# A decoder layer's opening: x scaled and transposed with the identity, first adaLN sums on TensorE, silu(c) later

## The chip, the core and the metric

The kernel runs on one core of a Trainium2 chip. The metric is the device time of one execution in microseconds. The trace names the engines PE (TensorE matmul; PEld its weight loads), DVE (VectorE), ACT (ScalarE), POOL (GpSimd) and SP (SyncE, which issues the transfers here). All data are float32, or float32 in the form that TensorE multiplies in fewer passes (`fp32r`).

## The reference, cut to what matters

One layer, 512 tokens, width 2048, batch 1. The part that the change touches is the modulated norm at its start:

```python
mod = jax.nn.silu(c) @ w_ada + b_ada                 # (1, 6144)
shift, scale, gate = jnp.split(mod[:, None, :], 3, axis=-1)
h = rms_norm(x, norm_w) * (1.0 + scale) + shift      # (1, 512, 2048)
proj = h @ w_in
```

Behind it stand sliding-window attention with sinks, a gated DeltaNet branch, their merge, and `x + gate * (y @ w_out)`. All of these read `proj`, and so `h`; the change does not touch them.

## The kernel before, in words

`startup` makes `h` transposed, 16 blocks of 128 channels by 512 tokens, and multiplies each block as soon as it is there with the first weights (`w_st`: two v tiles, one for beta and alpha, four k tiles). Its steps:

- **Loads.** SP issues all transfers in program order. x comes in four groups of 128 tokens (`xt`), the row of c spread over all partitions (`scb`, printed as `silu_cb`), the adaLN weights (`wa`) two tiles of 1 MiB for each block: `loads[kt, 0]` for shift and `loads[kt, 1]` for scale. `xt` and `wa` share six buffers, so a `wa` load can wait for an earlier tile to be used up. The weights `raw` have two buffers of their own.
- **Norm and transpose.** For each token group ScalarE squares x and sums (L467), VectorE takes the root of the mean in ten small instructions (L469 and `rsqrt`, L64), scales the identity by it into `dg` (L472), and TensorE multiplies x by `dg`, which scales and transposes in one (L477). VectorE and ScalarE in turn copy the result out of PSUM into `xnT` (L480, L482).
- **silu(c).** `silu(c)` in column form (`scr`) is the stationary operand for TensorE. The row form `scb` is made after the second group by a tanh on ScalarE (L486) and one instruction on VectorE (L487).
- **adaLN sums** (`ada_sums`, L420). For an even block the shift comes from 16 small TensorE matmuls (L428), a copy (L433) and a small matmul with `pick` (L434); the weights are laid out by `layout` for that. All others are dot products on VectorE (L437), 2.28 us each.
- **h** (`adaln`, L441). Two small VectorE instructions make shift and scale (`sh`, L445 and L449), ScalarE makes `h` (L454) and its high part `hh` (L455), VectorE the low part `hl` (`low`, L458).
- **Products.** Each weight half is split in the same way into `whi` (L61) and `wlo` (L62). `mm3` multiplies high by high, low by high and high by low (L255 to L257), so a block has 21 matmuls.

The loop over blocks `kt` (L504) writes down, in this order: `adaln(kt+1)`, the loads of block kt+3, the sums of block kt+2, `low(kt+1)`, the products of block kt. The order on each engine is not this order: a planner in the framework takes instructions by priority as they become ready by its own costs, and then each engine runs its list in order. `behind` (L259) adds an edge that makes the planner put one instruction after another on the same engine, without a wait at run time. After the loop the stage `delta_keys` begins, whose matmuls are named `mm`.

Of the kernel before, what the change touches and what calls it, by code (L numbers as in the profile page):

```python
# [7 lines left out]
F32 = mybir.dt.float32  # L8
F32R = mybir.dt.float32r
I32 = mybir.dt.int32  # L10
AF = mybir.ActivationFunctionType
ALU = mybir.AluOpType
# [4 lines left out]
P = 128  # L17
T = 512
D = 2048
KT = D // P  # L20
NTB = T // P
EPS = 1e-6
# [23 lines left out]
class Layer:  # L46
# [321 lines left out]
    def startup(self, st):  # L368


        tc, nc, a, const = self.tc, self.nc, self.a, self.const
        sp = st.enter_context(tc.tile_pool(name="st1", bufs=1, reuse_waits="tile"))
        s2 = st.enter_context(tc.tile_pool(name="st2", bufs=2, reuse_waits="tile"))
        pa = st.enter_context(tc.tile_pool(name="st_acc", bufs=1, space=PSUM, reuse_waits="tile"))
        acc, loads = {}, {}

        def load_ada(kt):
            for j in range(2):
                wa = s2.tile([P, D], F32, tag="wa", name="wa", bufs=6)
                nc.sync.dma_start(out=wa, in_=a["w_ada_ss"][kt, j])  # L380
                loads[kt, j] = wa

        consts = self.consts()
        xts = []
        scb = sp.tile([P, D], F32, name="silu_cb")
        for tb in range(NTB):
            xt = s2.tile([P, D], F32, tag="wa", name="xt", bufs=6)
            nc.sync.dma_start(out=xt, in_=a["x"][tb * P : (tb + 1) * P, :])
            xts.append(xt)
            if tb < 2:  # L390
                next(consts)
            if tb == 1:
                nc.sync.dma_start(out=scb, in_=a["c_row"].partition_broadcast(P))
        load_ada(0)
        next(consts)
        self.prime()
        load_ada(1)
        load_ada(2)
        next(consts)
# [6 lines left out]
        scr = sp.tile([P, KT, 32], F32, name="silu_cr")  # L406
        nc.vector.tensor_copy(out=scr, in_=self.sc.unsqueeze(2).to_broadcast([P, KT, 32]))
        pick = sp.tile([P, 1], F32, name="pick")
        nc.vector.memset(pick, 0.0)
        for g in range(4):  # L410
            nc.vector.memset(pick[32 * g : 32 * g + 1], 1.0)
        bn = sp.tile([P, KT], F32, name="bn")
        nc.vector.scalar_tensor_tensor(
            out=bn, in0=self.b_ada[:, KT : 2 * KT], scalar=1.0, in1=self.norm_w, op0=ALU.add, op1=ALU.mult
        )
        ssq = sp.tile([P, NTB], F32, name="xssq")
        xnT = sp.tile([P, KT, T], F32, name="xnT")
        ada = pa.tile([P, T], F32, name="ada")

        def ada_sums(kt):  # L420


            t = acc[kt] = s2.tile([P, 2], F32, tag="acc", name="acc")
            if kt % 2 == 0:
                w = loads[kt, 0].rearrange("p (k n) -> p k n", k=KT)
                for k in range(4):
                    for g in range(4):
                        nc.tensor.matmul(  # L428
                            ada[32 * g : 32 * g + 32, 0:P], lhsT=scr[:, 4 * k + g, :], rhs=w[:, 4 * k + g, :],
                            start=k == 0, stop=k == 3,  # L430
                        )
                sb = s2.tile([P, P], F32, tag="adas", name="adas", bufs=1)
                nc.scalar.copy(out=sb, in_=ada[:, 0:P])  # L433
                nc.tensor.matmul(ada[:, P : P + 1], lhsT=sb, rhs=pick, start=True, stop=True)  # L434
            for j in range(1 - kt % 2, 2):
                wa = loads[kt, j]
                nc.vector.scalar_tensor_tensor(  # L437
                    out=wa, in0=wa, scalar=0.5, in1=scb, op0=ALU.mult, op1=ALU.mult, accum_out=t[:, j : j + 1]
                )

        def adaln(kt):  # L441

            t = acc[kt]
            sh = s2.tile([P, 2], F32, tag="sh", name="sh")
            nc.vector.tensor_scalar(  # L445
                out=sh[:, 0:1], in0=t[:, 0:1] if kt % 2 else ada[:, P : P + 1], scalar1=self.b_ada[:, kt : kt + 1],
                scalar2=None, op0=ALU.add,
            )
            nc.vector.tensor_scalar(  # L449
                out=sh[:, 1:2], in0=t[:, 1:2], scalar1=self.norm_w[:, kt : kt + 1], scalar2=bn[:, kt : kt + 1],  # L450
                op0=ALU.mult, op1=ALU.add,
            )
            h32 = s2.tile([P, T], F32, tag="h32", name="h32")
            nc.scalar.activation(h32, xnT[:, kt, :], AF.Identity, scale=sh[:, 1:2], bias=sh[:, 0:1])  # L454
            nc.scalar.copy(out=self.hh[:, kt, :], in_=h32)  # L455
            return h32

        def low(kt, h32):  # L458
            nc.vector.tensor_tensor(
                out=self.hl[:, kt, :], in0=h32, in1=self.hh[:, kt, :].bitcast(F32), op=ALU.subtract  # L460
            )

        n = 0
        for tb in range(NTB):
            xt = xts[tb]
            junk = self.hl[:, 4 * tb : 4 * tb + 4, :].rearrange("p k t -> p (k t)")
            nc.scalar.activation(junk, xt, AF.Square, accum_out=ssq[:, tb : tb + 1])  # L467
            ms = sp.tile([P, 1], F32, tag="ms", name="ms", bufs=2)
            nc.vector.tensor_scalar(out=ms, in0=ssq[:, tb : tb + 1], scalar1=1.0 / D, scalar2=EPS, op0=ALU.mult, op1=ALU.add)  # L469
            r = self.rsqrt(sp, ms, 1, "xr")  # L470
            dg = s2.tile([P, P], F32, tag="dg", name="dg")
            nc.vector.tensor_scalar(out=dg, in0=self.ident, scalar1=r, scalar2=None, op0=ALU.mult)  # L472
            for q in range(4):
                i = n % 7
                ps = pa.tile([P, 4, P], F32, tag=f"x{i}", name="xtp") if i < 3 else self.psc.tile([P, 4, P], F32, tag="sc", name="xtp")
                for c in range(4):
                    nc.tensor.matmul(ps[:, c, :], lhsT=xt[:, (4 * q + c) * P : (4 * q + c + 1) * P], rhs=dg, start=True, stop=True)  # L477
                dst = xnT[:, 4 * q : 4 * q + 4, tb * P : (tb + 1) * P]
                if q % 2:
                    nc.vector.tensor_copy(out=dst, in_=ps)  # L480
                else:
                    nc.scalar.copy(out=dst, in_=ps)  # L482
                n += 1
            if tb == 1:
                thb = sp.tile([P, D], F32, name="silu_t")
                nc.scalar.activation(thb, scb, AF.Tanh, scale=0.5)  # L486
                nc.vector.scalar_tensor_tensor(out=scb, in0=thb, scalar=1.0, in1=scb, op0=ALU.add, op1=ALU.mult)  # L487

        def products(kt, parts):
            f, l = kt == 0, kt == KT - 1  # L490
            wh, wl = parts
# [3 lines left out]

        ada_sums(0)
        low(0, adaln(0))
        ada_sums(1)
        acc_v = [pa.tile([P, T], F32, tag=f"x{i}", name=f"v{i}") for i in range(2)]
        acc_ba = pa.tile([2 * VH, T], F32, tag="x2", name="ba")  # L500
# [1131 lines left out]
def layout(i):  # L1632
# [8 lines left out]
    o["c_row"] = f(i["c"].reshape(D))  # L1641
    ss = w_ada[:, : 2 * D].T.reshape(2, KT, P, D).transpose(1, 0, 2, 3).copy()
    ss[0::2, 0] = ss[0::2, 0].reshape(-1, P, KT, P).transpose(0, 3, 2, 1).reshape(-1, P, D)
    o["w_ada_ss"] = ss
    o["w_ada_gate"] = f(w_ada.reshape(KT, P, 3, D)[:, :, 2])
    o["b_ada"] = f(i["b_ada"][0].reshape(48, P).T)
# [65 lines left out]
```

## Time and profile before

| what | us |
|---|---|
| median of 3 runs | 2878.47 (2870.41 to 2881.5) |
| profiled execution | 2872.04, span 2870.2 |
| first matmul of a transposition (L477) | 10.27 |
| first product of block 0 (L255) | 32.93 |
| first product of block 1 | 41.54 |
| first product of block 2 | 48.30 |
| first product of block 15 | 136.46 |
| first `mm` of the next stage | 141.38 |

The positions are counted from the start of the span. Names are those of the program without buffer numbers. In a timeline a row gives start, duration, engine, line, operation, written and read tile, shapes, a count, and in brackets the idle time before it with what ended it. Durations of matmuls are modelled and overlap, so the spacing of their starts is the better measure.

### The profile page before, as it was taken

To read this page: it belongs to the slowest core of one execution; us is meant where nothing else is said; L and a number is where in the kernel's file an instruction comes from. 1 tells how busy PE (TensorE), PEld (TensorE's weight loads), DVE (VectorE), ACT (ScalarE), POOL (GpSimd) and SP (SyncE) were. 2 spreads that over 40 slices of the span, in tenths; PEclk is the share of its full clock that TensorE was granted. 3 is DMA by queue.
4 is the path that set the end of the run, shared out by engine and by line. 5 is a ranking of instruction groups with operands and counts; after the bars stand their busy time and mean duration, and the time that the engine had idled before them with its cause. 6 is when DMAs were issued, how large, how long until landed. Compare 5 with 4: busy or idle time off the path is not lost.

```text
span 2870.2 us, 38671 instructions
## 1 busy us (share of the span) xinstructions
PE 2820.4 (98%) x14396; PEld 2314.6 (81%) x14396; DVE 1969.6 (69%) x3174; ACT 1188.4 (41%) x2382; POOL 141.6 (5%) x124
## 2 busy tenths in 40 slices
PE   7899999999999999999999999999999999999999
PEld 6588888877877778888788888888888888878887
DVE  7776776868768766778676666665656776664576
ACT  4356443234444343433433333333334454433443
POOL 0001000100001000001000000000000000000000
PEclk9999999999999999999999999999999999999999
DMA  9777864322252343456777676666646887885784
GB/s 398 289 250 235 257 231 143 112 89 90 80 159 81 110 151 99 134 170 233 236 261 246 229 241 232 235 236 228 231 171 226 288 314 258 295 281 175 245 317 165
DMA packets 227727, 604.28 MB, mean 211 GB/s; under 512 B 76081, under 2 KB 102193, under 8 KB 187089
## 3 DMA queue, kind: packets, MB, share of 16 engines
q1 hardware_dynamic: 227538, 601.81, 62.0%
q8 instruction: 113, 1.85, 0.3%
q14 instruction: 76, 0.62, 0.1%
HBM read 481.32 MB, written 118.17 MB: 209 GB/s over the span
## 4 chain that ended last, share of the span: by engine, by line
PE 87%; DVE 5%; DMA 3%; ACT 2%; issue 1%; SPq 0%; POOL 0%; DVEq 0%; POOLq 0%; ACTq 0%
PE mm L255 20%; PE mm L257 20%; PE mm L256 20%; PE m L256 5%; PE m L255 5%; PE m L257 5%; DVE wa L437 1%; DVE wlo L62 1%; PE pv L933 1%; DMA E<-g_rows 1%; PE S L1389 1%; PE pod L952 1%; PE O L1440 1%; PE pP L296 1%; ACT sm L1413 1%
## 5 line engine op out<-in xcount | busy, mean ns | idle before, releaser
L255 PE MATMUL mm<-hh,whi 128*128 128x512 f32 x2784 | 1130.1, 406 | 2.8 <-ACT mth L285 2.8
L257 PE MATMUL mm<-hh,wlo 128*128 128x512 f32 x2784 | 1089.5, 391 | 0.0
L256 PE MATMUL mm<-hl,whi 128*128 128x512 f32 x2784 | 1086.9, 390 | 0.0
L62 DVE TENSOR_TENSOR wlo<-raw,whi 128x1024 fp32r<-128x1024 f32 (+1 forms) x532 | 655.2, 1232 | 425.0 <-ACT whi L61 409.6
L61 ACT CAST whi<-raw 128x1024 fp32r<-128x1024 f32 (+1 forms) x532 | 555.4, 1045 | 848.6 <-PE mm L256 612.2
L255 PEld LDWEIGHTS mm<-hh,whi 128*128 128x128 f32 x2784 | 523.5, 188 | 113.6 <-issue 9.2
L257 PEld LDWEIGHTS mm<-hh,wlo 128*128 128x128 f32 x2784 | 522.6, 188 | 113.6 <-issue 0.5
L256 PEld LDWEIGHTS mm<-hl,whi 128*128 128x128 f32 x2784 | 524.0, 188 | 100.4 <-issue 1.4
L1198 DVE TENSOR_TENSOR q<-q,q 128x1024 f32<-128x1024 f32 x96 | 124.5, 1297 | 0.2 <-DMA q<-in_w_od 0.2
L748 ACT ACTIVATE E<-E,neg_g 128x128 f32<-128x128 f32 x256 | 82.1, 393 | 88.7 <-POOL E L742 88.6
L777 DVE TENSOR_TENSOR atmp<-A 128x62 f32<-128x62 f32 (+30 forms) x124 | 109.7, 884 | 0.5
L785 DVE TENSOR_TENSOR A<-A,atmp 128x62 f32<-128x62 f32 (+30 forms) x124 | 109.1, 880 | 0.4
L880 POOL TENSOR_TENSOR qe<-qe,yq 128x512 f32<-128x512 f32 x32 | 50.9, 1608 | 940.2 <-DMA qe<-eg_rows 624.3
L953 ACT COPY osb<-pod 128x256 f32<-128x256 f32 x64 | 23.8, 372 | 149.9 <-PE pod L952 149.9
L742 POOL TENSOR_SCALAR_AFFINE_SELECT E<-E 128x512 f32<-128x512 f32 x64 | 60.0, 950 | 430.7 <-DMA E<-g_rows 307.2
L935 ACT COPY vn<-pv 128x256 f32<-128x256 f32 x64 | 23.8, 372 | 120.8 <-PE pv L933 120.8
L1413 ACT ACTIVATE sm<-sm,mx,rs 128x256 f32<-128x256 f32 (+1 forms) x128 | 71.7, 562 | 3.5 <-DVE mx L1408 3.5
L604 DVE SCALAR_TENSOR_TENSOR yv<-mm,convh,yv 128x511 f32<-128x511 f32 (+2 forms) x96 | 71.4, 743 | 1.2
L940 DVE TENSOR_SCALAR vs<-vn,kd 128x128 f32<-128x128 f32 x96 | 23.1, 283 | 60.6 <-ACT vn L935 60.6
L437 DVE SCALAR_TENSOR_TENSOR wa<-wa,silu_cb 128x2048 f32<-128x2048 f32 x24 | 54.8, 2283 | 0.0
L963 DVE SCALAR_TENSOR_TENSOR S<-S,egl,pod 128x128 f32<-128x128 f32 x64 | 19.3, 343 | 50.8 <-ACT junk L956 50.8
L609 ACT ACTIVATE th<-yv 128x512 f32<-128x512 f32 x32 | 20.1, 628 | 72.7 <-DVE yv L604 72.7
(427 smaller groups left out, 3684.4 us busy)
## 6 DMA issues: line engine op xcount, KB each, us to landing
raw<-in_w_ch SPq DMA_DIRECT2D x158, 1024.0 KB
wa<-in_w_ada_ss SPq DMA_DIRECT2D x32, 1024.0 KB
q<-in_w_od SPq DMA_DIRECT2D x64, 512.0 KB
g_d<-q SPq DMA_DIRECT2D x64, 512.0 KB
raw<-g_d SPq DMA_DIRECT2D x32, 1024.0 KB
raw<-in_w_od SPq DMA_DIRECT2D x24, 1024.0 KB
gw<-in_w_ada_gate SPq DMA_DIRECT2D x16, 1024.0 KB
E<-g_rows SPq DMA_DIRECT2D x64, 256.0 KB
```

The costliest lines, as they stand in the source:

```text
L61: self.nc.scalar.copy(out=hi, in_=src)
L62: self.nc.vector.tensor_tensor(out=lo, in0=src, in1=hi.bitcast(F32), op=ALU.subtract)
L255: nc.tensor.matmul(ps, lhsT=wh, rhs=xh, start=first, stop=False)
L256: nc.tensor.matmul(ps, lhsT=wh, rhs=xl, start=False, stop=False)
L257: self.last_mm = nc.tensor.matmul(ps, lhsT=wl, rhs=xh, start=False, stop=last)
L437: nc.vector.scalar_tensor_tensor(out=wa, in0=wa, scalar=0.5, in1=scb, op0=ALU.mult, op1=ALU.mult, accum_out=t[:, j : j + 1])
L604: nc.vector.scalar_tensor_tensor(out=y[:, s:], in0=ps[:, : T - s], scalar=w[:, j : j + 1], in1=y[:, s:], op0=ALU.mult, op1=ALU.add)
L748: self.nc.scalar.activation(E[:, c, :], E[:, c, :], AF.Exp, bias=self.neg_g[:, c, h : h + 1])
L777: eng.tensor_tensor(out=t, in0=A[:, m : m + 1, m + 1 :].to_broadcast([P, m, n]), in1=A[:, :m, m : m + 1].to_broadcast([P, m, n]), op=ALU.mult,
L785: self.behind(eng.tensor_tensor(out=A[:, :m, m + 1 :], in0=A[:, :m, m + 1 :], in1=t, op=ALU.add))
L1198: self.behind(nc.vector.tensor_tensor(out=q[f], in0=q[x], in1=q[y], op=ALU.add))
L1413: nc.scalar.activation(t, t, AF.Exp, scale=r[:, h : h + 1], bias=mx[:, h : h + 1], accum_out=den[:, h : h + 1])
```

## The change

- The row of c is loaded after the first two weight loads instead of after the second x group; `b_ada` and `norm_w` are loaded ahead of the first `wa`.
- Two token groups share one chain for the root. x itself is scaled in its buffer by VectorE, and TensorE transposes it with the unscaled identity. PSUM of groups 2 and 3 is copied out by ScalarE alone.
- Block 0 takes both sums from TensorE, placed behind the last transpose; `layout` stores that tile accordingly. Before, its scale was summed on VectorE.
- `scb` becomes silu(c) after block 0's `hh` and `hl`, so the first VectorE sums are those of block 1.
- Both `sh` instructions move from VectorE to ScalarE.
- From block 4 on, `low(kt)` is placed behind the first VectorE sum of block kt+1.

```diff
--- before.py
+++ after.py
@@ -372,7 +372,7 @@
         sp = st.enter_context(tc.tile_pool(name="st1", bufs=1, reuse_waits="tile"))
         s2 = st.enter_context(tc.tile_pool(name="st2", bufs=2, reuse_waits="tile"))
         pa = st.enter_context(tc.tile_pool(name="st_acc", bufs=1, space=PSUM, reuse_waits="tile"))
-        acc, loads = {}, {}
+        acc, loads, sums, made = {}, {}, {}, {}
 
         def load_ada(kt):
             for j in range(2):
@@ -389,11 +389,10 @@
             xts.append(xt)
             if tb < 2:
                 next(consts)
-            if tb == 1:
-                nc.sync.dma_start(out=scb, in_=a["c_row"].partition_broadcast(P))
+        next(consts)
         load_ada(0)
-        next(consts)
         self.prime()
+        nc.sync.dma_start(out=scb, in_=a["c_row"].partition_broadcast(P))
         load_ada(1)
         load_ada(2)
         next(consts)
@@ -421,71 +420,73 @@
 
 
             t = acc[kt] = s2.tile([P, 2], F32, tag="acc", name="acc")
-            if kt % 2 == 0:
-                w = loads[kt, 0].rearrange("p (k n) -> p k n", k=KT)
+            for j in range(2 if kt == 0 else 1 - kt % 2):
+                w = loads[kt, j].rearrange("p (k n) -> p k n", k=KT)
+                o = 256 * j
                 for k in range(4):
                     for g in range(4):
-                        nc.tensor.matmul(
-                            ada[32 * g : 32 * g + 32, 0:P], lhsT=scr[:, 4 * k + g, :], rhs=w[:, 4 * k + g, :],
+                        ins = nc.tensor.matmul(
+                            ada[32 * g : 32 * g + 32, o : o + P], lhsT=scr[:, 4 * k + g, :], rhs=w[:, 4 * k + g, :],
                             start=k == 0, stop=k == 3,
                         )
+                        if kt == 0:
+                            self.behind(ins, last_tp)
                 sb = s2.tile([P, P], F32, tag="adas", name="adas", bufs=1)
-                nc.scalar.copy(out=sb, in_=ada[:, 0:P])
-                nc.tensor.matmul(ada[:, P : P + 1], lhsT=sb, rhs=pick, start=True, stop=True)
-            for j in range(1 - kt % 2, 2):
+                nc.scalar.copy(out=sb, in_=ada[:, o : o + P])
+                nc.tensor.matmul(ada[:, o + P : o + P + 1], lhsT=sb, rhs=pick, start=True, stop=True)
+            for j in range(2 if kt == 0 else 1 - kt % 2, 2):
                 wa = loads[kt, j]
-                nc.vector.scalar_tensor_tensor(
+                ins = nc.vector.scalar_tensor_tensor(
                     out=wa, in0=wa, scalar=0.5, in1=scb, op0=ALU.mult, op1=ALU.mult, accum_out=t[:, j : j + 1]
                 )
+                sums.setdefault(kt, ins)
 
         def adaln(kt):
 
             t = acc[kt]
             sh = s2.tile([P, 2], F32, tag="sh", name="sh")
-            nc.vector.tensor_scalar(
-                out=sh[:, 0:1], in0=t[:, 0:1] if kt % 2 else ada[:, P : P + 1], scalar1=self.b_ada[:, kt : kt + 1],
-                scalar2=None, op0=ALU.add,
+            nc.scalar.activation(
+                sh[:, 0:1], t[:, 0:1] if kt % 2 else ada[:, P : P + 1], AF.Identity, bias=self.b_ada[:, kt : kt + 1]
             )
-            nc.vector.tensor_scalar(
-                out=sh[:, 1:2], in0=t[:, 1:2], scalar1=self.norm_w[:, kt : kt + 1], scalar2=bn[:, kt : kt + 1],
-                op0=ALU.mult, op1=ALU.add,
+            nc.scalar.activation(
+                sh[:, 1:2], t[:, 1:2] if kt else ada[:, 256 + P : 257 + P], AF.Identity, scale=self.norm_w[:, kt : kt + 1], bias=bn[:, kt : kt + 1]
             )
             h32 = s2.tile([P, T], F32, tag="h32", name="h32")
             nc.scalar.activation(h32, xnT[:, kt, :], AF.Identity, scale=sh[:, 1:2], bias=sh[:, 0:1])
-            nc.scalar.copy(out=self.hh[:, kt, :], in_=h32)
+            made["h"] = nc.scalar.copy(out=self.hh[:, kt, :], in_=h32)
             return h32
 
         def low(kt, h32):
-            nc.vector.tensor_tensor(
+            ins = made["l"] = nc.vector.tensor_tensor(
                 out=self.hl[:, kt, :], in0=h32, in1=self.hh[:, kt, :].bitcast(F32), op=ALU.subtract
             )
+            if kt > 3 and kt + 1 in sums:
+                self.behind(ins, sums[kt + 1])
 
         n = 0
         for tb in range(NTB):
             xt = xts[tb]
             junk = self.hl[:, 4 * tb : 4 * tb + 4, :].rearrange("p k t -> p (k t)")
             nc.scalar.activation(junk, xt, AF.Square, accum_out=ssq[:, tb : tb + 1])
-            ms = sp.tile([P, 1], F32, tag="ms", name="ms", bufs=2)
-            nc.vector.tensor_scalar(out=ms, in0=ssq[:, tb : tb + 1], scalar1=1.0 / D, scalar2=EPS, op0=ALU.mult, op1=ALU.add)
-            r = self.rsqrt(sp, ms, 1, "xr")
-            dg = s2.tile([P, P], F32, tag="dg", name="dg")
-            nc.vector.tensor_scalar(out=dg, in0=self.ident, scalar1=r, scalar2=None, op0=ALU.mult)
-            for q in range(4):
-                i = n % 7
-                ps = pa.tile([P, 4, P], F32, tag=f"x{i}", name="xtp") if i < 3 else self.psc.tile([P, 4, P], F32, tag="sc", name="xtp")
-                for c in range(4):
-                    nc.tensor.matmul(ps[:, c, :], lhsT=xt[:, (4 * q + c) * P : (4 * q + c + 1) * P], rhs=dg, start=True, stop=True)
-                dst = xnT[:, 4 * q : 4 * q + 4, tb * P : (tb + 1) * P]
-                if q % 2:
-                    nc.vector.tensor_copy(out=dst, in_=ps)
-                else:
-                    nc.scalar.copy(out=dst, in_=ps)
-                n += 1
-            if tb == 1:
-                thb = sp.tile([P, D], F32, name="silu_t")
-                nc.scalar.activation(thb, scb, AF.Tanh, scale=0.5)
-                nc.vector.scalar_tensor_tensor(out=scb, in0=thb, scalar=1.0, in1=scb, op0=ALU.add, op1=ALU.mult)
-
+            if tb % 2 == 0:
+                continue
+            ms = sp.tile([P, 2], F32, tag="ms", name="ms", bufs=2)
+            nc.vector.tensor_scalar(out=ms, in0=ssq[:, tb - 1 : tb + 1], scalar1=1.0 / D, scalar2=EPS, op0=ALU.mult, op1=ALU.add)
+            r = self.rsqrt(sp, ms, 2, "xr")
+            for b in (tb - 1, tb):
+                xt, u = xts[b], b % 2
+                nc.vector.tensor_scalar(out=xt, in0=xt, scalar1=r[:, u : u + 1], scalar2=None, op0=ALU.mult)
+                for q in range(4):
+                    i = n % 7
+                    ps = pa.tile([P, 4, P], F32, tag=f"x{i}", name="xtp") if i < 3 else self.psc.tile([P, 4, P], F32, tag="sc", name="xtp")
+                    for c in range(4):
+                        last_tp = nc.tensor.transpose(ps[:, c, :], xt[:, (4 * q + c) * P : (4 * q + c + 1) * P], self.ident)
+                    dst = xnT[:, 4 * q : 4 * q + 4, b * P : (b + 1) * P]
+                    if q % 2 and b < 2:
+                        nc.vector.tensor_copy(out=dst, in_=ps)
+                    else:
+                        nc.scalar.copy(out=dst, in_=ps)
+                    n += 1
         def products(kt, parts):
             f, l = kt == 0, kt == KT - 1
             wh, wl = parts
@@ -495,6 +496,11 @@
 
         ada_sums(0)
         low(0, adaln(0))
+        thb = sp.tile([P, D], F32, name="silu_t")
+        self.behind(nc.scalar.activation(thb, scb, AF.Tanh, scale=0.5), made["h"])
+        self.behind(
+            nc.vector.scalar_tensor_tensor(out=scb, in0=thb, scalar=1.0, in1=scb, op0=ALU.add, op1=ALU.mult), made["l"]
+        )
         ada_sums(1)
         acc_v = [pa.tile([P, T], F32, tag=f"x{i}", name=f"v{i}") for i in range(2)]
         acc_ba = pa.tile([2 * VH, T], F32, tag="x2", name="ba")
@@ -1641,6 +1647,7 @@
     o["c_row"] = f(i["c"].reshape(D))
     ss = w_ada[:, : 2 * D].T.reshape(2, KT, P, D).transpose(1, 0, 2, 3).copy()
     ss[0::2, 0] = ss[0::2, 0].reshape(-1, P, KT, P).transpose(0, 3, 2, 1).reshape(-1, P, D)
+    ss[0, 1] = ss[0, 1].reshape(P, KT, P).transpose(2, 1, 0).reshape(P, D)
     o["w_ada_ss"] = ss
     o["w_ada_gate"] = f(w_ada.reshape(KT, P, 3, D)[:, :, 2])
     o["b_ada"] = f(i["b_ada"][0].reshape(48, P).T)
```

## The prediction

> **What bounds the kernel now.** I read the page first. TensorE is the engine that fills the span.
>
> ```profile
> PE 2820.4 (98%) x14396; PEld 2314.6 (81%) x14396; DVE 1969.6 (69%) x3174; ACT 1188.4 (41%) x2382; POOL 141.6 (5%) x124
> ```
>
> All edits lie in the startup stage. I take as its end the first `mm` matmul of the next stage, at 141.38 us; after that TensorE has no idle time worth naming (50.00 busy of 50.00 below), so a shift of that point should reach the end of the kernel one for one. The windows say what is near its limit inside the stage.
>
> ```profile
> core 0: us, PE busy (x) PEld busy (x) DVE busy (x) ACT busy (x) POOL busy (x), PEclk, DMA share, GB/s
> 5.00:55.00 50.00, 37.75 (x296) 32.37 (x296) 37.34 (x91) 24.18 (x34) 0.00 (x0) 0.97 1.01 418
> 55.00:120.00 65.00, 55.04 (x340) 39.25 (x340) 52.70 (x67) 20.91 (x32) 0.00 (x0) 1.00 0.97 380
> 120.00:125.00 5.00, 5.00 (x52) 3.63 (x51) 2.92 (x6) 2.48 (x4) 0.00 (x0) 1.00 0.16 67
> 68.95:82.56 13.61, 11.62 (x78) 8.30 (x77) 10.77 (x16) 4.61 (x8) 0.00 (x0) 1.00 0.96 368
> 150.00:200.00 50.00, 50.00 (x249) 41.50 (x248) 37.79 (x71) 27.42 (x77) 4.48 (x5) 1.00 0.77 255
> ```
>
> From 55 us on nothing is full: the transfers slow from 418 to 380 GB/s, VectorE has 10.77 us of work in a 13.61 us pair of blocks, and busy TensorE is overstated by overlapping records. So it is a loop of waits, and the chain shows one turn of it (start, us, what).
>
> ```profile
> 68.73 0.22 DVE sh L445
> 68.95 2.22 DVE wa L437 x2
> ...
> 71.19 0.28 DVE sh L449
> ...
> 71.50 0.82 ACT h L454
> 72.32 0.79 ACT whi L61
> ...
> 73.13 1.03 DVE wlo L62
> 74.16 2.21 DVE wa L437 x2
> 76.37 0.62 DVE hl L459
> ...
> 77.03 0.50 PE v L256
> ...
> 80.51 1.01 PE ada L428 x32
> ...
> 82.34 0.22 DVE sh L445
> ```
>
> 82.34 - 68.73 = 13.61 us for two blocks. VectorE stands in order: `sh` at L445 waits there for the adaLN sum on TensorE, with the next `wa` sum behind it; and `sh` at L449 waits behind a 2.2 us `wa` sum, although its own sum was done before, so ScalarE's `h` is late, then `hh`, then `hl`, then TensorE. The waits from 55 to 137 us name the links of the turn (total, times, longest).
>
> ```profile
> ACT h L454 <- DVE sh L449: 51.0, 12, 6.0
> ...
> DVE hl L459 <- ACT hh L455: 7.7, 5, 1.5
> DVE wlo L62 <- ACT whi L61: 6.2, 7, 1.8
> ...
> DVE sh L445 <- PE ada L434: 4.7, 6, 2.1
> ```
>
> **The loop after the change.** The loop keeps its products and its sums from block 1 on; what changes is that both `sh` go to ScalarE. VectorE loses 0.22 + 0.28 us twice per pair, say 1.0 of its 10.77, and with them the waits of `sh` (4.7/6 = 0.8 per pair); `h` starts when its sums are done, so `hl` finds `hh` ready (7.7/6 = 1.3). The `wlo` wait (6.2/6 = 1.0) I leave in. VectorE then needs 9.8 + 1.0 = 10.8 us per pair. ScalarE gains four small instructions: 0.2 us as the smallest ACTIVATE below, and 0.1 more for each per-partition operand (`h`, which has two, takes 0.82 where the cast of the same size, `hh`, takes 0.62 by its row in the opening below). That is 1.4 us on a 4.61 us load; it is off the path.
>
> What TensorE needs when nothing makes it wait is two blocks from 48.30 on, with one adaLN sum between them, and the price of a cold start is in block 1:
>
> ```profile
> 41.54 0.62 PE L255 MATMUL v<-hh,whi 128*128 128x512 f32 x1 [2.49 <-ACT hh L455]
> ...
> 43.24 0.63 PE L255 MATMUL k<-hh,whi 128*128 128x512 f32 x1
> 43.67 0.63 PE L256 MATMUL v<-hl,whi 128*128 128x512 f32 x1
> ...
> 48.30 0.61 PE L255 MATMUL v<-hh,whi 128*128 128x512 f32 x2
> ...
> 59.13 0.39 PE L257 MATMUL k<-hh,wlo 128*128 128x512 f32 x1
> ...
> 141.38 0.39 PE L255 MATMUL mm<-hh,whi 128*128 128x512 f32 x1
> ```
>
> 59.13 + 0.23 - 48.30 = 11.06 us per pair. One block is (11.06 - 1.01)/2 = 5.0. Block 1 took 48.30 - 41.54 = 6.76, or 1.8 more: after the idle stretch its matmuls start 0.43 us apart instead of 0.23. That idle stretch stays after the change, and so does the 1.8. From the start of block 1 TensorE needs 1.8 + 7 x 11.06 + 5.0 = 84.2 us; now it takes 141.38 - 41.54 = 99.8. The gain of a fed TensorE is 15.6 us.
>
> The transfers set another floor. The last `wa` lands at 120.8 us now (0.335 MB of the 120 to 125 row). At 418 GB/s the 65 us at 380 shrink by 65 x (1 - 380/418) = 5.9, so it lands at 114.9; after that come one sum 2.22, `sh` 0.4, `h` 0.82, `hh` 0.62 and block 15: 123.9 us. That is close under the other path, so the two will get in each other's way. I add 0.4 us per pair for this and for the new order on ScalarE, where `sh` of an even block waits for the sum on TensorE with `h`, `hh` and the next `whi` queued behind it: 7 x 0.4 = 2.8. Bounds: nothing, and the whole 15.6 if the wait only moves.
>
> **The opening before block 1.** Rows of the opening, and three prices from elsewhere in the trace (the transposes of `pr`; `gate_bc`, a scaling of 128x2048 by a per-partition value; and the small ACTIVATE):
>
> ```profile
> 10.37 0.20 ACT L403 ACTIVATE cth<-ch 128x16 f32<-128x16 f32 x1
> ...
> 10.50 0.15 DVE L469 TENSOR_SCALAR ms<-xssq 128x1 f32<-128x1 f32 x1 [0.28 <-ACT hl L467]
> ...
> 10.95 1.91 ACT L486 ACTIVATE silu_t<-silu_cb 128x2048 f32<-128x2048 f32 x1 [0.38 <-DMA silu_cb<-in_c_row]
> ...
> 12.90 0.28 DVE L472 TENSOR_SCALAR dg<-ident,xry 128x128 f32<-128x128 f32 x1
> ...
> 14.09 0.69 DVE L480 COPY xnT<-xtp 128x512 f32<-128x512 f32 x1 [0.91 <-PE xtp L477]
> ...
> 14.70 2.28 DVE L487 SCALAR_TENSOR_TENSOR silu_cb<-silu_t,silu_cb 128x2048 f32<-128x2048 f32 x1
> ...
> 15.72 1.92 ACT L467 ACTIVATE hl<-xt 128x2048 fp32r<-128x2048 f32 x1
> ...
> 21.32 7.38 PE L477 MATMUL xtp<-dg,xt 128*128 128x128 f32 x64 [1.65 <-issue]
> ...
> 27.84 0.59 ACT L482 COPY xnT<-xtp 128x512 f32<-128x512 f32 x1 [1.20 <-PE xtp L477]
> ...
> 40.87 0.62 ACT L455 CAST hh<-h 128x512 fp32r<-128x512 f32 x1
> ...
> 157.80 0.44 PE pr L590 x4
> ...
> L1615 DVE TENSOR_SCALAR gate_bc<-gw,silu_c x1: 1187/1187/1187, 151.2 to 151.2; 128x2048 f32<-128x2048 f32 x1
> ```
>
> Transposing: 32 matmuls took 7.38 us; a transpose takes 0.11, so 64 take 7.0 where two batches of 32 took 14.8 or more. Removed too: the `dg` (4 x 0.28) and two of four root chains (10.50 to 12.86 by the rows of `ms` and `dg`, 2.4 each). Added on VectorE: four scalings of 1.19. The row of c leaves its place after the second x, where it landed at 10.95, and goes behind the two `raw` loads on SP's queue; both groups behind it move up by 2.5 us (1 MiB at 418 GB/s), to about 10.95 and 13.4. It is still ahead of the `wa` loads that wait for x's buffers, and its bytes are the same.
>
> Now the path. The fourth square ends at 13.4 + 2.0 = 15.4, or 17.7 if two evictions stay queued ahead of it on ScalarE (as the third square at 15.72 shows). Then the second roots 2.4, two scalings 2.4, the last 16 transposes 1.8: 22.0 to 24.3. VectorE's four evictions of groups 0 and 1 (0.69 each) fall among these: up to 2.8 more. Evictions of groups 2 and 3 all stand on ScalarE, 8 x 0.59 = 4.7 against 3.5 of transposes, which adds 1.2. The first block now has two sums on TensorE, held behind the last transpose: 2 x 1.01, two copies and two small matmuls of some 0.3 each, `sh` 0.4, `h` 0.82, `hh` 0.62, together 5.1. `hh` of block 0 is ready between 27 and 33.5 (the latter with two or three `whi` casts of 0.79 ahead of it); I take 30.5, near the middle.
>
> But block 1 hangs on the row silu(c), now made only after `hh`: tanh 1.91, the product 2.28, two sums 2 x 2.22, `sh` 0.4, `h` 0.82, `hh` 0.62, 0.2 of gaps: 10.7, and 1.0 more if a `wlo` stands between. So block 1 starts at 41.2 to 42.2; I take 41.5, which is where it starts now. **The faster opening is spent on waiting for silu(c).** Bounds 37.7 and 45.2.
>
> [...]
>
> **Sum.** End of the stage: 41.5 + 84.2 + 2.8 = 128.5, which is 12.9 us before 141.4. The profiled execution took 2872.0 us around a span of 2870.2, so it would take 2859.1. It lies 6.4 under the median of the runs shown, 2878.5; from the median it comes to 2865.6, and I say 2865.5.
>
> **Rivals.** (a) *Transfers decide, and the opening does save time:* block 1 starts at 38 or so, the stage ends at the floor of 123.9, and the gain is 17.5: 2861. For it: the transfers have a slot free earlier, and 418 was held for 50 us. Against: silu(c).
> (b) *Cold opening:* TensorE is at half rate through transposes and first sums. `hh` comes at 33.5, block 1 at 44.2, the end at 131.2: gain 10.2, 2868.3. For it: the first 32 matmuls now span more than the later 7.38. Against: evictions hide part.
> (c) *The wait only moves:* pairs stay near 13 us because ScalarE, in order, holds `whi` and `h` behind `sh` as VectorE did. 7 x (13 - 11.06) = 13.6 instead of 2.8: gain 2.1, 2876.4. Against: ScalarE has 9 us idle per pair.
> (d) *Slower:* the sum of an even block is placed behind the block before it on TensorE, so that copy, small matmul, `sh`, `h`, `hh` (0.3 + 0.3 + 0.7 + 0.82 + 0.62 = 2.7) stand between blocks in every pair: 11.06 + 2.7 = 13.8, and with block 1 at 45.2 the stage ends at 45.2 + 84.2 + 7 x 2.7 = 148.3, 6.9 late: 2885.4. It decides as soon as this gap and the late block 1 add up to more than 15.6. Against: now the sum runs a whole block of 5.0 ahead.
>
> **Chances.** Forecast 0.45, (a) 0.22, (b) 0.12, (c) 0.15, (d) 0.06. What a measurement tells from no change is about 0.5%, 14.4 us: the forecast lies 1.5 short of it, and a median of such runs (2870 to 2881 now) moves by several us. Faster: four tenths of the forecast, nine of (a), three of (b), one of (c): 0.18 + 0.20 + 0.04 + 0.02 = 0.44. Slower needs (d) and its spread, 0.04. The rest, 0.52, is within. The forecast's own range is 2859 to 2872. For 8 in 10 I take 2854, (a) with a median 7 lower, to 2879, beyond (c).
>
> **What would show it.** Right: pairs near 11.5 us, no `hl` wait on `hh`, transfers above 400 GB/s until they end near 115 to 118, block 1 at 41 with an idle TensorE before it that ends on `hh` and, behind it, the silu(c) product. Wrong: pairs still above 12.5, with waits of `h` on TensorE's sum; block 1 far from 41.5; or a first `mm` that comes early while the span does not follow.

## The result and the profile after

| | before | after |
|---|---|---|
| median of 20 runs each, us | 2876.55 (2870.41 to 2887.08) | 2869.80 (2863.37 to 2875.28) |
| ratio, 95% interval | | 0.9976, 0.9967 to 0.9984 |
| first product of block 0 | 32.93 | 35.52 |
| first product of block 1 | 41.54 | 46.13 |
| a pair of blocks, in the middle of the loop | 13.62 | 12.05 |
| first `mm` | 141.38 | 137.67 |

The change gains 6.75 us, 0.24% (4.6 to 9.5 us by the interval). The start of the next stage moves by 3.7 us: the loop over the blocks gives 8.3 us back, and the opening costs 4.6.

The same windows as before, now of the kernel after, and below them one pair of blocks:

```profile
core 0: us, PE busy (x) PEld busy (x) DVE busy (x) ACT busy (x) POOL busy (x), PEclk, DMA share, GB/s
5.00:55.00 50.00, 31.60 (x217) 26.06 (x218) 30.14 (x53) 26.42 (x42) 0.00 (x0) 0.86 0.96 388
55.00:120.00 65.00, 60.54 (x426) 44.85 (x424) 52.70 (x53) 30.50 (x58) 0.00 (x0) 1.00 0.99 406
120.00:125.00 5.00, 5.00 (x34) 3.84 (x23) 2.85 (x6) 3.59 (x7) 0.00 (x0) 1.00 0.11 44
...
83.10:95.15 12.05, 11.30 (x81) 8.38 (x84) 9.87 (x11) 5.69 (x12) 0.00 (x0) 1.00 1.00 405
```

From 55 us on the transfers run at 406 instead of 380 GB/s. In the opening they fall from 418 to 388, and the granted clock (the column PEclk) from 0.97 to 0.86. That column shows 1.00 also where the trace has no record of the clock: the first record is a rise at 20.24 us in the kernel after, and at 14.47 before. VectorE now has 9.87 us of work in a pair of 12.05 us, so it still waits for 2.2.

The chain of waits through one pair (start, us, what) tells for what:

```profile
83.10 1.01 PE ada L428 x32
...
84.93 0.26 ACT sh L448
85.19 0.27 ACT sh L451
85.47 0.78 ACT whi L61
86.24 0.72 ACT h L455
86.96 0.79 ACT whi L61
...
91.01 0.61 DVE hl L460
...
95.15 1.01 PE ada L428 x32
```

Before, the chain ran through `sh` on VectorE. Now it runs through ScalarE: the first `sh` of an even block waits there for the sum on TensorE, the second and the casts `whi` stand behind it, and VectorE's `wlo`, the next sum and `hl` follow late. The waits from 55 to 137 us agree (total, times, longest):

```profile
DVE wlo L62 <- ACT whi L61: 14.7, 13, 2.2
...
DVE hl L460 <- ACT hh L456: 2.0, 1, 2.0
```

The wait of `wlo` for `whi` has grown from 6.2 to 14.7 us; that of `hl` for `hh` has fallen from 7.7 to 2.0.

The opening, as a timeline of the kernel after:

```profile
14.34 6.57 PE L483 MATMUL xtp<-ident,xt 128*128 128x128 f32 x32 [14.34 <-DVE xt L478]
...
15.97 1.91 ACT L470 ACTIVATE hl<-xt 128x2048 fp32r<-128x2048 f32 x1
...
18.66 0.16 DVE L474 TENSOR_SCALAR ms<-xssq 128x2 f32<-128x2 f32 x1
...
22.91 2.48 DVE L478 TENSOR_SCALAR xt<-xt,xry 128x2048 f32<-128x2048 f32 x2
24.34 5.00 PE L483 MATMUL xtp<-ident,xt 128*128 128x128 f32 x32 [3.44 <-DVE xt L478]
...
29.28 1.08 PE L428 MATMUL ada<-wa,silu_cr 128*32 128x128 f32 x32
30.04 0.94 ACT L61 CAST whi<-raw 128x832 fp32r<-128x832 f32 x1
...
30.83 0.33 ACT L435 COPY adas<-ada 128x128 f32<-128x128 f32 x1
...
31.21 0.38 PE L436 MATMUL ada<-pick,adas 128*128 128x1 f32 x2 [0.85 <-ACT adas L435]
...
31.52 1.08 PE L428 MATMUL ada<-wa,silu_cr 128*32 128x128 f32 x32
...
34.85 0.62 ACT L456 CAST hh<-h 128x512 fp32r<-128x512 f32 x1
35.37 1.91 ACT L500 ACTIVATE silu_t<-silu_cb 128x2048 f32<-128x2048 f32 x1
...
37.31 2.29 DVE L502 SCALAR_TENSOR_TENSOR silu_cb<-silu_t,silu_cb 128x2048 f32<-128x2048 f32 x1 [1.12 <-ACT silu_t L500]
...
46.13 0.51 PE L255 MATMUL v<-hh,whi 128*128 128x512 f32 x1 [2.13 <-ACT hh L456]
```

The fourth square starts at 15.97, behind an eviction. The second roots take 22.91 - 18.66 = 4.25 us, because VectorE's evictions, which wait for TensorE, stand among them. The two adaLN sums of block 0 run one after the other: the second starts at 31.52, behind the small matmul of the first in TensorE's list; that matmul waits for the copy, which stands behind a `whi` on ScalarE. So `hh` of block 0 ends at 35.47, and block 1 starts 10.66 us later, at the end of the chain tanh, product, two sums, `sh`, `h`, `hh`.

### The profile page after: what moved, and what is told of

Same layout as the page of the kernel before. It is cut to its first block, busy times and chain, and to the rows that moved or that the text cites. A ratio compares the mean times of both kernels' runs of the same rounds, so it can differ in the third digit from the quotient of the medians.

```text
span 2872.5 us, 38612 instructions
## 1 busy us (share of the span) xinstructions
PE 2820.8 (98%) x14366; PEld 2314.3 (81%) x14366; DVE 1960.2 (68%) x3114; ACT 1200.5 (42%) x2419; POOL 144.3 (5%) x124
## 4 chain that ended last, share of the span: by engine, by line
PE 88%; DVE 4%; DMA 4%; ACT 3%; issue 1%; SPq 0%; POOL 0%; DVEq 0%; POOLq 0%; ACTq 0%
PE mm L255 21%; PE mm L257 20%; PE mm L256 20%; PE m L256 5%; PE m L257 5%; PE m L255 5%; PE pv L939 1%; DMA E<-g_rows 1%; PE pod L958 1%; PE S L1395 1%; PE O L1446 1%; PE pP L296 1%; ACT whi L61 1%; PE pod L957 1%; PE pp L929 1%
```

## The experiments

In the table, "first mm less block 1" is the loop; "median less first mm" is all that comes behind the stage. Positions are from one profile of each kernel.

| kernel | median, us | ratio to before, 95% | block 0 | block 1 | pair | first mm | median less first mm |
|---|---|---|---|---|---|---|---|
| before | 2876.55 | | 32.93 | 41.54 | 13.62 | 141.38 | 2735.2 |
| the change | 2869.80 | 0.9976 (0.9967 to 0.9984) | 35.52 | 46.13 | 12.05 | 137.67 | 2732.1 |
| before, `sh` on ScalarE | 2875.08 | 0.9995 (0.9986 to 1.0004) | 33.33 | 43.41 | 13.62 | 142.89 | 2732.2 |
| before, edge | 2879.96 | 1.0016 (1.0006 to 1.0026) | 32.96 | 41.55 | 14.08 | 144.39 | 2735.6 |
| before, `sh` and edge | 2864.70 | 0.9963 (0.9951 to 0.9976) | 33.71 | 44.00 | 12.05 | 135.54 | 2729.2 |
| change without the edge | 2879.19 | 1.0009 (0.9998 to 1.0019) | 36.01 | 46.61 | 13.62 | 146.32 | 2732.9 |
| change, `sh` on VectorE | 2881.89 | 1.0017 (1.0008 to 1.0026) | 37.13 | 47.64 | 14.1 | 150.18 | 2731.7 |
| change, row of c early | 2865.74 | 0.9959 (0.9947 to 0.9972) | 33.79 | 42.67 | 12.05 | 131.17 | 2734.6 |
| the same, `whi` first | 2860.75 | 0.9948 (0.9933 to 0.9963) | 37.68 | 45.68 | 11.01 | 128.40 | 2732.4 |
| before, `sh`, edge, `whi` first | 2860.14 | 0.9955 (0.9942 to 0.9967) | 33.95 | 44.34 | 11.01 | 130.33 | 2729.8 |
| change, weights two ahead | 2875.64 | 1.0002 (0.9992 to 1.0013) | 36.05 | 46.66 | 12 to 16 | 149.53 | 2726.1 |

The last column stays within 2726 and 2736 while the first `mm` moves by 22 us, so a shift of the stage's end does reach the end of the kernel, one for one as near as this can tell.

### Both `sh` on ScalarE, and nothing else

```diff
-            nc.vector.tensor_scalar(
-                out=sh[:, 0:1], in0=t[:, 0:1] if kt % 2 else ada[:, P : P + 1], scalar1=self.b_ada[:, kt : kt + 1],
...
+            nc.scalar.activation(
+                sh[:, 0:1], t[:, 0:1] if kt % 2 else ada[:, P : P + 1], AF.Identity, bias=self.b_ada[:, kt : kt + 1]
...
```

> The kernel before with one edit: both sh instructions on ScalarE. Theory A (the loop's gain comes from sh alone, the opening of the change costs some of it): pairs of blocks at about 12.0 us instead of 13.6, block 1 still at 41.5, first mm near 132, time about 9 us under the kernel before, so lower than the changed kernel (6.7 under). Rival B (the loop needs the opening or the added edge for its gain): pairs near 13.6, first mm near 141, time within 2 us of before. Rival C (ScalarE in order is as bad as VectorE): pairs near 13, gain 3 to 4 us.

The pairs stay at 13.62 us, and the time is not told apart from before. VectorE's order in the loop of this kernel, in its timeline:

```profile
78.34 2.29 DVE L437 SCALAR_TENSOR_TENSOR wa<-wa,silu_cb 128x2048 f32<-128x2048 f32 x1
...
80.67 0.39 ACT L448 ACTIVATE sh<-acc,bn,norm_wT 128x1 f32<-128x1 f32 x1 [2.52 <-DVE wa L437]
...
82.59 0.69 DVE L457 TENSOR_TENSOR hl<-h,hh 128x512 fp32r<-128x512 f32 x1 [1.96 <-ACT hh L453]
```

The sum at 78.34 is the scale of the odd block itself: `sh` at 80.67 waits for it. `sh`, `h` and `hh` can only follow it, and `hl`, next in VectorE's list, waits 1.96 us for them. The kernel before has the same order, with `sh` on VectorE:

```profile
77.01 2.28 DVE L437 SCALAR_TENSOR_TENSOR wa<-wa,silu_cb 128x2048 f32<-128x2048 f32 x1
...
79.34 0.27 DVE L449 TENSOR_SCALAR sh<-acc,norm_wT,bn 128x1 f32<-128x1 f32 x1
...
81.15 0.69 DVE L459 TENSOR_TENSOR hl<-h,hh 128x512 fp32r<-128x512 f32 x1 [1.53 <-ACT hh L455]
```

The time that `sh` took came back as waiting. Over a pair VectorE waited 2.8 us before (1.53 here, 0.50 at the other `sh`, 0.74 for a `whi`); now it waits 3.7 (1.96 here, 1.23 and 0.47 for two `whi`, the first of which stands behind `sh` on ScalarE).

### The change without the edge

```diff
-            if kt > 3 and kt + 1 in sums:
-                self.behind(ins, sums[kt + 1])
```

> The changed kernel without the edge that puts hl behind the next block's first sum. After the run with sh alone (pairs still 13.62), theory G: sh on ScalarE frees VectorE, but hl of an odd block then stands right behind its own sum and waits 2 us for hh; the edge puts one more sum between, and that is the loop's gain. Expected by G: pairs back at 13.5 to 13.7, a wait of hl on hh of 2 us per pair, block 1 near 46, first mm near 146, time 3 to 5 us over the kernel before. Rival H (the opening is what shortens the pairs, the edge does nothing): pairs at 12.0 to 12.2, time as the changed kernel (2870).

Pairs at 13.62, the first `mm` at 146.32, and no gain is left. So it is the same with the new opening, and the edge is needed.

### The edge with `sh` on VectorE, behind both openings

First the change with both `sh` put back on VectorE (the reverse of the diff above):

> The changed kernel with both sh back on VectorE, the rest as changed. Theory A: pairs back near 13.6 us, block 1 at about 46, first mm near 146 to 147, time 4 to 6 us over the kernel before. Rival B (opening and edge carry the gain): pairs at 12.5 or less, first mm at 139 or earlier, time at or under the kernel before.

Then the kernel before with the edge alone:

```diff
+                sums.setdefault(kt, ins)
...
+            if kt > 3 and kt + 1 in sums:
+                self.behind(ins, sums[kt + 1])
```

> The kernel before with the edge alone: hl of a block is placed behind the first VectorE sum of the next block, both sh stay on VectorE. It completes the square of the two loop edits (none 13.62 us per pair, sh on ScalarE alone 13.62, edge with sh on VectorE about 14.1 behind the new opening, both 12.05). Theory G (only both together help, since sh on VectorE still stands behind that sum, and the edge lets hl come one sum later without filling a wait): pairs 13.6 to 14.2, first mm at 141 to 146, time 2876 to 2882. Rival (the edge itself carries the gain, and the about 14.1 came from the new opening): pairs at most 12.6, first mm at most 137, time about 2868.

Both have pairs of 14.1 us and are slower than before, by 0.17% with the new opening and 0.16% with the old one. With the new opening the first `mm` comes at 150.18, later than the 146 to 147 expected. In the timeline of the kernel with the edge alone:

```profile
97.55 0.22 DVE L446 TENSOR_SCALAR sh<-ada,b_adaT 128x1 f32<-128x1 f32 x1 [2.73 <-PE ada L434]
...
97.69 2.28 DVE L437 SCALAR_TENSOR_TENSOR wa<-wa,silu_cb 128x2048 f32<-128x2048 f32 x1
...
99.89 0.69 DVE L460 TENSOR_TENSOR hl<-h,hh 128x512 fp32r<-128x512 f32 x1
```

`hl` stands behind the sum at 97.69 as the edge wants. But that sum stands behind `sh` of the even block, which waits 2.73 us for TensorE in VectorE's list. The hole is where it was (before, 1.53 us at `hl` and 0.50 at the next `sh`), and `hl` is later.

### Both, with the opening of before

The two diffs above together, in the kernel before.

> The kernel before with both sh on ScalarE and the edge, its opening untouched: the loop's part of the change without the opening's. Theory G: pairs 12.05 from block 4 on, block 1 near 43.4 as with sh alone, first mm at 133 to 135, time 2867 to 2870, that is as fast as the changed kernel or faster by up to 4 us: the new opening has cost time. Rival H (the opening shortens the pairs): pairs 13.6, first mm near 142, time 2875.

Pairs of 12.05 us and 0.37% faster (2864.70 us, 2 us less than expected). The four cases of `sh` and edge are 13.62 (neither), 13.62 (`sh`), 14.1 (edge) and 12.05 (both): neither part is worth anything alone. In the kernel after one sees why:

```profile
93.74 2.29 DVE L439 SCALAR_TENSOR_TENSOR wa<-wa,silu_cb 128x2048 f32<-128x2048 f32 x1
...
93.86 0.39 ACT L451 ACTIVATE sh<-acc,bn,norm_wT 128x1 f32<-128x1 f32 x1 [2.52 <-DVE wa L439]
...
95.13 0.62 ACT L456 CAST hh<-h 128x512 fp32r<-128x512 f32 x1
...
95.95 0.69 DVE L460 TENSOR_TENSOR hl<-h,hh 128x512 fp32r<-128x512 f32 x1
```

While ScalarE makes `sh`, `h` and `hh` (93.86 to 95.75), VectorE does the next sum (93.74 to 95.95), and `hl` follows without a wait.

It also compares the openings: with both loop edits the old one reaches the first `mm` 2.1 us sooner (135.54 against 137.67), with `sh` alone 3.4 (142.89, 146.32), with the edge alone 5.8 (144.39, 150.18). The medians point the same way, by 5.1, 4.1 and 1.9 us, but in each pair the intervals of the ratios overlap. Part of it is the granted clock and not the opening: with the old opening block 1 comes at 41.5 where block 0 runs at full clock (before, and the edge alone: its matmuls start 0.23 us apart, and before shows a granted 1.00 from 33 to 39 us), and at 43.4 to 44.3 in the three kernels where block 0 starts at half clock (0.43 us apart; with both loop edits the trace shows 0.50 from 33 to 39 us). So the 4.6 us of the first table compare with a profile in which block 0 ran at full clock.

### The row of c early

The change, with the load of the row right behind x, the tanh ahead of the evictions of group 2, its product behind the last scaling of x, and the sums of block 1 ahead of block 0's `hl`:

```diff
+        nc.sync.dma_start(out=scb, in_=a["c_row"].partition_broadcast(P))
         next(consts)
         load_ada(0)
...
+            if tb == 1:
+                thb = sp.tile([P, D], F32, name="silu_t")
+                tanh = nc.scalar.activation(thb, scb, AF.Tanh, scale=0.5)
+                self.behind(tanh, ev)
...
+        ada_sums(1)
         low(0, adaln(0))
+        self.behind(made["l"], made["s"])
```

> The changed kernel with the row silu(c) made in the gap of ScalarE before the evictions of group 2, its load put right behind x, and the sums of block 1 ahead of hl and wlo of block 0. Theory A (block 1 hangs on the late row): block 0 stays near 35 to 36, block 1 follows it without a gap at about 42 instead of 46.1, first mm near 133.5, time 4 us under the changed kernel. Rival D (transfers are the floor: the last adaLN weights land at 120.5 in the changed kernel and decide the end): block 1 at 42 but first mm still at 136 to 138, time within 1.5 us of the changed kernel. Rival E (hh of block 1 waits for something else): block 1 stays past 45.

Block 1 starts at 42.67, right behind block 0's last matmul (42.44), instead of waiting 2.13 us for `hh`. From block 0 to block 1 it takes 8.88 us, 1.7 less than in the change (10.61). Another 1.7 come from block 0 itself, and these are no evidence for the edit: the second half of the transposes takes 3.68 us here and 5.00 in the change, and the kernel with the cast ahead, below, has the same opening as this one, takes 6.63 us for them and reaches block 0 only at 37.68:

```profile
24.50 6.63 PE L484 MATMUL xtp<-ident,xt 128*128 128x128 f32 x32 [3.52 <-DVE xt L479]
```

### Ordinary matmuls in place of the transposes

```diff
-                        last_tp = nc.tensor.transpose(ps[:, c, :], xt[:, (4 * q + c) * P : (4 * q + c + 1) * P], self.ident)
+                        last_tp = nc.tensor.matmul(ps[:, c, :], lhsT=xt[:, (4 * q + c) * P : (4 * q + c + 1) * P], rhs=self.ident, start=True, stop=True)
```

> The changed kernel with the 64 transposes written as ordinary matmuls with the identity. [...]

Block 0 is no sooner (36.82, for 35.52 in the change) and its matmuls still start 0.43 us apart, at a granted 0.50 from 39 to 43 us; in the change they do so at 0.50 from 36 to 40. So ordinary matmuls in place of the transposes do not take that slow start away. The length of the idle stretch ahead does not decide it either: TensorE is idle for 2.09 us ahead of block 0 here, and for 2.46 us in the kernel before, whose block 0 starts its matmuls 0.23 us apart at 1.00. The clock during the transposition does differ. Windows of one to three us (TensorE's busy time and records, granted clock, DMA share, GB/s): the change,

```profile
23.00:24.00 1.00, 0.00 (x0) 0.82 1.02 434
24.00:25.00 1.00, 0.66 (x3) 0.50 0.99 418
...
27.00:28.00 1.00, 1.00 (x11) 0.97 1.03 434
```

the kernel with the row early, and after it the kernel with ordinary matmuls:

```profile
24.00:27.00 3.00, 3.00 (x30) 1.00 1.02 428
```

```profile
24.00:27.00 3.00, 3.00 (x29) 1.00 1.00 423
```

In the change the clock falls to 0.50 during the 3.44 us in which TensorE waits for the second roots and a scaling, and the transposes run slowly for the first 2.7 us behind them (13 in 2.65 us, then 20 in 2.00). The ordinary matmuls take so long, 16.86 us from 14.25 on, that the gap closes, and the clock shows 1.00 until 36 us. With the row early the gap is 3.53 us and the clock stays at 1.00; so the same gap costs something in one kernel and nothing in the other.

### The cast ahead of the copy

The kernel with the early row, and on ScalarE the copy of an even block's TensorE sum (and with it the `sh` of the shift) placed behind that block's `whi`:

```diff
-                nc.scalar.copy(out=sb, in_=ada[:, o : o + P])
+                made["sb", kt] = nc.scalar.copy(out=sb, in_=ada[:, o : o + P])
...
+            if kt % 2 and 3 <= kt < KT - 1:
+                self.behind(made["sb", kt + 1], self.his[kt + 1])
```

> The kernel with the early row (2865.7, first mm 131.2, pairs 12.05) and one more edge: on ScalarE the copy of an even block's TensorE sum stands behind the first of the two whi casts, so that the cast does not wait for that sum. Theory F (VectorE's 2.2 us per pair of waiting for whi is what keeps pairs from 11.06): pairs fall to 11.3 to 11.7, first mm at 128 to 129.5, time 2862 to 2864. Rival I (hl is late because h and hh are, not because wlo is): the wait for whi shrinks but pairs stay at 12.0, first mm near 131. Rival D (transfers): pairs at 12.0 and VectorE waits for adaLN weights.

Then the same two loop edits and this one with the opening of before:

> The opening of the kernel before, with both loop edits of the change and, as in the run before this one, the copy of an even block's TensorE sum placed behind that block's whi on ScalarE. Theory F (what is left in a pair is the whi that stands behind sh on ScalarE) with theory O (the old opening is not slower than the changed one): pairs 11.0, block 1 at 43 to 44, first mm at 126 to 129, time 2857 to 2862. Rival (the 11.0 was reached only because the early row of c also fed VectorE sooner; with the old opening the pairs stay above 11.6): first mm at 131 or later, time 2864.

Both have pairs of 11.01 us. In the windows of one pair, first with the early row, then with the old opening, TensorE has no idle time left, at 426 and 427 GB/s:

```profile
80.01:91.02 11.01, 11.01 (x80) 8.53 (x77) 9.98 (x10) 5.94 (x12) 0.00 (x0) 1.00 1.01 426
```

```profile
76.04:87.05 11.01, 11.01 (x78) 8.52 (x76) 9.98 (x11) 5.94 (x11) 0.00 (x0) 1.00 1.01 427
```

ScalarE's order in the first of them is now this:

```profile
90.21 0.87 ACT L61 CAST whi<-raw 128x832 fp32r<-128x832 f32 x1
...
91.32 0.89 ACT L61 CAST whi<-raw 128x832 fp32r<-128x832 f32 x1
...
93.97 0.26 ACT L449 ACTIVATE sh<-ada,b_adaT 128x1 f32<-128x1 f32 x1 [1.76 <-PE ada L436]
```

The one edge moved both casts ahead of the `sh` that waits for TensorE. So the last 1.04 us of a pair of the change was the casts behind that `sh`. These are the two fastest kernels, 0.5% under before; they are not told apart. The old opening's first `mm` is 1.3 us later than the 126 to 129 expected: from the start of block 1 to that of block 5 it takes 26.6 us (44.34 to 70.95), where the early row takes 23.3 (45.68 to 69.01). No run shows why.

### Weights split two halves ahead

```diff
+        self.split_half()
+        self.split_half()
         for kt in range(KT):
```

> The changed kernel with the weight halves split two blocks ahead instead of one inside the loop, which puts the whi casts ahead of the sh of even blocks on ScalarE. Theory F (pairs take 12.05 instead of 11.06 because whi stands behind sh, which waits for the sum on TensorE; VectorE waits 2.2 us per pair for whi): that wait goes, pairs fall to 11.1 to 11.5, first mm near 133 to 134, time 3 to 5 us under the changed kernel. Rival D (transfers set the 12.05): pairs stay at 12.0 with the wait moved to the sums, time as the changed kernel.

The whole gain is lost. In the waits of this kernel (60 to 130 us),

```profile
DVE wlo L62 <- ACT whi L61: 21.7, 10, 4.6
...
ACT whi L61 <- PE k L256: 5.4, 4, 2.7
```

the cast, asked for earlier, waits in four places for TensorE to free its buffer, and what follows on ScalarE stands behind it. Elsewhere the cast still stands behind the copy of a TensorE sum: at 117.61 that copy has waited 2.93 us, the cast comes at 118.01, and `wlo` has waited 4.57 us for it. The clock takes part as well: a mean of 0.92 from 55 to 120 us, where the change has 1.00, and matmuls 0.43 us apart from 91.97 to 97.09. That more buffers would mend this was not tried.

### The change, profiled a second time

> The change as it is, profiled a second time. The first mm repeats within 1 us of 137.7 and a pair takes 12.0 to 12.1 us, since waits in order set them. If the span minus the first mm changes by some us between two profiles of one and the same program, while the stage repeats, then the 2.3 us by which the profiled change was longer than the profiled kernel before is the clock and not the opening. If the span repeats at 2872 to 2873 and the clock too, the later stages cost more after the change, and that is open.

The first `mm` comes at 138.30, 0.6 after the first profile. The span is 2864.9 us at a mean clock of 0.997, after 2872.5 at 0.996. Behind the first `mm` that is 2734.8 and 2726.6 us for one and the same program; before it was 2728.8. The profiled span of the change that is 2.3 us longer than that of before lies within this scatter, and nothing in a later stage need explain it. The second profile shows the half clock longer, from 22 to 29 us:

```profile
22.00:23.00 1.00, 0.00 (x0) 0.60 1.01 426
...
29.00:30.00 1.00, 1.00 (x16) 0.99 1.03 426
```

and its second 32 transposes take 6.34 us.

## Why the prediction was right in its number and wrong in its parts

The median, 2869.80, lies 4.3 us from the 2865.5 forecast and inside the range, and within 0.5% was the likeliest case. The gain is half the size, 6.75 for 13.0, and the first `mm` comes 9.2 us later than the 128.5 of the sum. The two terms share that evenly. That the median came as near as 4.3 us is in part luck: 1.9 us come from the median of before, which is lower over 20 runs than over the 3 that were known, and 3.0 from a gain that has no place in the trace.

**The loop, 87.0 forecast, 91.5 measured** (46.13 to 137.67). The term "I add 0.4 us per pair" for friction was mis-sized: it is 12.05 - 11.06 = 1.0 in the middle of the loop, with 1.9 in the second pair. The mechanism named with it, `sh` waiting on TensorE's sum with "the next `whi` queued behind it", is what the chain shows, and the run with the cast first takes it away. Rival (c), the wait moves to ScalarE, thus holds in its mechanism, at 1.0 instead of 1.9 us a pair.

**The step that says why the loop gains is wrong.** It said that `sh` at L449 waits behind a foreign sum, and that without `sh` on VectorE "`hl` finds `hh` ready". The sum was the block's own, as the rows at 77.01 and 78.34 show, and moving `sh` alone gains nothing. What makes `hl` find `hh` ready without a new wait elsewhere is the edge together with `sh` on ScalarE, and for the edge the prediction has no term at all, although the change lists it. The size came out near because what was costed, VectorE's work (9.8 forecast, 9.87 measured) and TensorE's need (11.06, and 11.01 in the best runs), is independent of that story.

**The opening, block 1 at 41.5 forecast, 46.13 measured.** The chain from `hh` to block 1 was right: 10.7 forecast, 10.66 measured, and the early row shows that block 1 hangs on it. The step that failed is "`hh` of block 0 is ready between 27 and 33.5": it is ready at 35.47. The late bound leaves out part of the prediction's own terms. Its late end of the transposes is 24.3; with the evictions (2.8 and 1.2), the 5.1 behind them and three casts (2.4) that it lists beside it, it comes to 35.8, and the forecast took 30.5. What was paid: the roots take 4.25 us for 2.4, since VectorE's evictions stand among them and wait for TensorE, and the square ends at 18.0 for 17.7. Behind the scalings, the transposes last 3.9 us for 1.8, with the half clock in 1.7 of them, so they end at 29.3. From there to `hh` it is 6.2 for 5.1: the copy of the first sum stands behind a cast. (The prediction's 12.86 for the end of the first roots is 12.90 in its own row; nothing hangs on it.)

**Rival (b), the cold opening,** is borne out for the transposes and not for the sums. The first 32 run at half rate too, though the clock column shows 1.00 there:

```profile
14.00:20.00 6.00, 5.66 (x27) 1.00 1.01 419
...
24.00:27.00 3.00, 2.65 (x13) 0.50 1.00 423
27.00:29.00 2.00, 2.00 (x20) 0.98 1.02 434
```

27 records in 5.66 us and 13 in 2.65 are the same pace, half that of 20 in 2.00; it ends with the first recorded rise, at 20.24 us. The evictions wait for these transposes, and the second roots stand among the evictions. The adaLN sums that follow are not slow (1.08 us for 32 records at 29.28, as for a sum of the loop at 70.97). The clock rose at 20.24 us, when TensorE had run nothing but transposes, and it came back to 0.97 at 27 to 28 us, when nothing but transposes had run since 24.34. What ran slowly were the first transposes, which started after 14.34 us without a matmul, and those behind the gap of 3.44 us.

**Rival (a)** did not come: the opening saves nothing, and the transfers, at 406 GB/s, thin out at 120 to 121 us as before, not at 115 to 118. **Rival (d)** did not come either: block 1 was even later than its 45.2, but the sum of an even block still runs ahead of the block before it (95.08 for block 10, and block 9 at 96.09).

Of the gain of the medians, 3.7 us have their place in the trace. The interval of the gain, 4.6 to 9.5 us, does not reach down to that. But the 3.7 compare one profile of each kernel, and block 0 of before ran at full clock in its one; the other 3 us also lie within the scatter of the last column of the table. They are given no cause.

## What to carry to other kernels

In a loop of in-order engines, a wait at an instruction is removed by giving its engine something to do before it, not by making the engine lighter: here a lighter VectorE gained nothing, one place in the list gained nothing, and the two together 1.6 us a pair. Before crediting a moved instruction, find out whether what it waits for is its own input, and cost every ordering edge in the diff as an edit of its own. When a chain goes to another engine, look at once for what now stands behind it there: the next microsecond of a pair was two casts that stood behind an instruction waiting for TensorE.

## What the runs showed of the hardware that was not expected

- The half clock of the transposition lasted 3.42 us in one profile of the change and 6.82, twice that, in the other. In the first it fell at 23.64 (a mean of 0.82 over 23 to 24, between 1.00 and 0.50, is full clock for 0.64 us) and rose at 27.06 (0.97 over 27 to 28). In the second it fell at 22.20 (0.60 over 22 to 23) and rose at 29.02 (0.99 over 29 to 30). In the kernel with the row early, and no cast moved, the clock stayed at 1.00 through a gap as long (3.53 us). What decides between these cases is not shown.
- At such a clock the second 32 transposes took 5.00 and 6.34 us in the two profiles of the change. In two kernels with the early row, whose opening is the same, they took 3.68 us at 1.00 and 6.63 at 0.50 from 24 to 30 us. A difference of 3 us in the opening, from one profile each, is therefore not evidence for an edit.
- At a granted 1.00, in the kernel with the early row, 32 transposes take 3.68 us, 0.115 us each, near the 0.11 that the prediction took from later rows. The first 32 of the change take 6.57, although the clock column shows 1.00: 27 of them are as far apart as those at a granted 0.50. Where the trace has no clock record yet, only the spacing tells.
